# Value rows in idle strips, a later normaliser step and a weight piece in a place of its own

## The chip, the cores and the metric

The kernel runs on one core of one Trainium2 chip. The metric is the device time of one execution in microseconds (us), lower is better. Engines are named as in the profile: PE (TensorE, matrix products), DVE (VectorE), ACT (ScalarE), POOL (GpSimd) and SP (SyncE, which issues nearly all DMAs). Each engine takes its instructions in the order of its own program; an instruction waits on semaphores that other engines and DMAs raise.

## The reference

One inference step of a one-layer decoder with 1,024 channels. A prompt of 512 tokens and 8 single sample tokens go through the same weights, 520 columns in all. One wide projection feeds a matrix-memory branch (mLSTM, four heads, key width 128, value width 256) and a sliding-window attention branch; both are gated and merged, projected, normalised, and go through a SwiGLU feed-forward block and a second normalisation.

```
z = x @ w_in                      # qk, mv, gates i/f, mo, aq, ak, av, gm, ga
qk = silu(causal_dwconv(qk, state_conv));  q, k = split(qk)
C_new = decay * C + i * k v^T;   n_new = decay * n + i * k     # per head
h = (q C) / max(|q n|, exp(-m)); h = rmsnorm(h)
y_m = sigmoid(mo) * h * g;       y_a = window_attention(aq, ak, av, sinks)
x = LN(ALPHA x + (sigmoid(gm) y_m + sigmoid(ga) y_a) @ w_out)
g, u = split(x @ w_gate_up);     ffn = (silu(g) * u) @ w_down
y = LN(ALPHA x + ffn + sigmoid(x @ w_ple_gate) * (p @ w_ple))
```

The prompt starts from an empty state and is done in chunks. Each of the 8 sample tokens has a state matrix C (128 x 256 for each head) and a normaliser n that are read, updated and written back; the convolution rows and the window caches are outputs too.

## The kernel before

Activations lie transposed, channels on partitions, 520 columns of which the first 8 are the samples. Every fp32 product is three matmuls: operands are split into a high and a low part (`split`: the high part by ACT at L218, the low part by DVE or POOL at L219), and high x high, high x low and low x high are summed in PSUM (L245). Weights come in blocks of up to 1 MB into a ring `raw` of two; each piece of a block (`prep_next`, L189) is split into the rings `whi` and `wlo`, three buffers each, unless `dest` names a place for it.

The projection runs in steps t, each 128 output channels: 48 matmuls on PE, then an evacuation. Steps 0 to 7 are the convolved q and k, 8 to 15 the memory values (`ev_mv`), 16 and 17 attention keys and values, 18 to 25 attention queries, then the gates. `ev_mv` copies a value block into the ring `stg` of two buffers of 520 columns (ACT, L984), transposes it on PE (L987, L992), and copies the prompt part (DVE, L988) and the sample part (L996) out of PSUM; after every second block it stores the sample rows to a scratch tensor `vsd` in DRAM (SP, L998).

Work beside the projection is queued in `sd`: `sd.add(steps, a, b)` spreads steps over t = a to b. What matters here:

- `conv_out` (L967), t 8 to 10: transposes the eleven convolution rows, copies them into two `stg` buffers and stores them with four DMAs (L974, L975).
- `smlstm_prep` (L1095), t 8 to 10: the sample normaliser. It reads n, transposes it (L1099), waits for `wdb`, a broadcast of gate factors through DRAM (L913), forms the new normaliser on DVE (L1102 to L1106), transposes it back (L1109), copies (L1111) and stores it (L1113).
- `ml0` to `ml3`: the prompt's memory. `ml0` broadcasts gate rows into the strips S0 to S7 (520 columns each, two for each head); `ml1` reads them in an exponential (ACT, L1054). When the last head's exponentials are done the strips are idle.
- `sm0`, `sm1`, `sm2`: sample states, eight groups (h, g) of four states of head h. `sm0` reads the states (L1120) and the broadcast value rows from `vsd` (L1121, 512 KB) into two buffers of the ring `big` (four buffers, shared with attention and other work). `sm1` scales the value rows by the key (ACT, L1141), adds the decayed state (DVE, L1142), splits the result, and multiplies it by the query on PE (L1148); SP stores the new states (L1152).
- `at1` to `at3`, `sattn`: window attention, on the same engines at the same time.

The feed-forward part begins with two column blocks of `w_gate_up` that are used directly, in eight pieces `k_gu` to `k_gu + 7`; pieces 3 and 4 have places of their own in a late tile, the others use the rings. The first pieces run while the first normalisation is finished, over half of the columns and then over the other half (the loop over `pb4`); beside the end of that loop DVE and ACT form sums of rows and their splits `tf` (L1490 to L1496) for the next stage.

The program is written in this order, but each engine's order is set by a scheduler that simulates the program as it is written; `tc.issue_after` (in `after`, L448) holds a step's instructions behind a named one.

Of the kernel before, what the change touches and what calls it, by code (L numbers as in the profile page):

```python
# [17 lines left out]
P = 128  # L18
# [32 lines left out]
def tile_hybrid_step(  # L51
# [915 lines left out]
    def conv_out():  # L967
        for g in range(2):
            ps = pss()
            for i in range(4):  # L970
                T.transpose(ps[:11, i * P : (i + 1) * P], cvo[:, 4 * g + i, :], ident)
            ost = ring("stg", NT, 2)
            V.tensor_copy(ost[:11, :512], ps[:11, :])
            nc.sync.dma_start(o_convs[0, :, 2, g * 512 : (g + 1) * 512], ost[:NS, :512])  # L974
            nc.sync.dma_start(o_convp[0, 0, :, g * 512 : (g + 1) * 512], ost[NS:11, :512])  # L975
            yield
# [4 lines left out]
    def ev_mv(f, pss2):  # L981
# [6 lines left out]
        V.tensor_copy(  # L988
            vaug()[:, :, f // 2, (f % 2) * P : (f % 2 + 1) * P], ps.rearrange("p (c d) -> p c d", c=NCH)
        )  # L990
# [125 lines left out]
    def sm0(hg):  # L1116
        h, g = hg
        Ct = big()[:, :1024].rearrange("p (b d) -> p b d", b=4)
        vb = big()[:, :1024].rearrange("p (b d) -> p b d", b=4)
        nc.sync.dma_start(Ct, st_C[0, 4 * g : 4 * g + 4, h].rearrange("b k d -> k b d"))  # L1120
        nc.sync.dma_start(  # L1121
            vb, vsd[4 * g : 4 * g + 4, h * DV : (h + 1) * DV].partition_broadcast(P)
        )
        late_t["sm", hg] = (Ct, vb)

    def sm1(hg):
# [12 lines left out]
        for i in range(4):  # L1139
            b = 4 * g + i  # L1140
            S.activation(vb[:, i, :], vb[:, i, :], AF.Copy, scale=kws[:, h, b : b + 1])  # L1141
            V.scalar_tensor_tensor(  # L1142
                Ct[:, i, :], Ct[:, i, :], wdb[:, h, 1, b : b + 1], vb[:, i, :], ALU.mult, ALU.add
            )
            cc = [ring("gt", 264, 5)[:, :DV] for _ in range(2)]
            split(cc[0], cc[1], Ct[:, i, :], G)
            for x in range(2):
                T.matmul(  # L1148
                    pn[:40, :DV], rr(qz[:, b, :]), rr(cc[x]),
                    start=(b == 0 and x == 0), stop=(b == NS - 1 and x == 1),  # L1150
                )
# [26 lines left out]
    mxhi = []  # L1178
    mxlo = []

    def ev_ga(f, pss2):
        if f == 0:
            mxhi.extend(v3(slab(3)))
# [37 lines left out]
    sd.add(gen_steps(smlstm_prep()), t_mv, t_mv + 2)  # L1221
# [63 lines left out]
    dest[k_gu + 4] = (sub8(T6, 2), sub8(T6, 3))  # L1285

# [134 lines left out]
    with tc.manual_schedule(engines={E.PE, E.DVE, E.Pool, E.Activation}):  # L1421
# [40 lines left out]
        ts[4, 0] = ev_g(pg[4], n0)  # L1462
        c1, n1 = HALVES[1]
# [555 lines left out]
```

## Time and profile before

| | before |
|---|---|
| median of 3 runs | 884.36 us (882.98 to 884.54) |
| profiled execution, its own time | 885.6 us |
| its span | 883.5 us (2.1 us lie around it) |
| mean granted PE clock | 0.995 |
| PE busy | 866.0 us (98%), 7,082 matmuls |
| DVE, ACT, POOL busy | 659.4, 475.5, 156.2 us |
| DMA | 103.69 MB, 117 GB/s over the span |

All busy times and stretches come from one profiled execution. A timeline row gives the start, the time that a run of like instructions took, the engine, line and operation, and in brackets the idle time of that engine just before and what ended it. Matmuls overlap, so the 0.28 us of one says little; 48 of the projection's matmuls take 5.76 us, 0.12 us each. What an engine other than PE waits for costs time only where PE then waits for it.

### The profile page before, as it was taken

How to read it: one execution, taken by the hardware profiler on the slowest of the kernel's cores; microseconds unless marked ns; L12 is line 12 of the kernel's file. 1: busy time of each engine (PE TensorE's matmuls, PEld its weight loads, DVE VectorE, ACT ScalarE, POOL GpSimd, SP SyncE). 2: the span in 40 equal slices, each digit the busy share in tenths (PEclk: the TensorE clock that was granted, in tenths of full speed). 3: DMA queues.
4: the chain of work that ended last, by engine and by line, in shares of the span. 5: the costliest groups of instructions: out<-in, count | busy, mean ns of one | idle time of the engine just before them, and what ended most of it. 6: DMA issues, size and time to landing. Idle time of an engine off the chain costs nothing.

```text
span 883.5 us, 18583 instructions
## 1 busy us (share of the span) xinstructions
PE 866.0 (98%) x7082; PEld 853.2 (97%) x7082; DVE 659.4 (75%) x1589; ACT 475.5 (54%) x1131; POOL 156.2 (18%) x315
## 2 busy tenths in 40 slices
PE   8999899999999999999999999999999999999996
PEld 7999899999999899999999999999999999999996
DVE  7788555688978676778876968898898875566337
ACT  6545254658777655566525846666666565222120
POOL 5441321115464411221012300000000000000002
PEclk9999999999999999999999999999999999999998
DMA  7642631336465451131520043333334337634212
GB/s 244 223 145 73 194 102 55 55 106 145 157 180 172 145 143 49 49 97 48 191 97 1 23 111 104 112 108 97 107 101 116 108 115 219 202 120 150 96 37 97
DMA packets 125369, 103.69 MB, mean 117 GB/s; under 512 B 7210, under 2 KB 121090, under 8 KB 125256
## 3 DMA queue, kind: packets, MB, share of 16 engines
q1 hardware_dynamic: 125136, 102.38, 38.7%
q8 instruction: 55, 0.90, 0.4%
q14 instruction: 34, 0.28, 0.1%
q10 hardware_dynamic: 144, 0.13, 0.0%
HBM read 91.14 MB, written 12.47 MB: 117 GB/s over the span
## 4 chain that ended last, share of the span: by engine, by line
PE 87%; DVE 5%; DMA 3%; ACT 2%; issue 1%; POOL 1%; SPq 0%; DVEq 0%; ACTq 0%
PE psm L245 41%; PE psm L1601 14%; PE pss L1601 11%; PE psm L228 5%; PE psm L1894 2%; PE psm L1918 2%; PE pss L684 2%; PE pss L737 1%; PE pss L721 1%; PE psm L1429 1%; DMA big<-vsd 1%; PE psm L468 1%; PE pss L1070 1%; PE pss L1074 1%; DMA wdb<-bcd 1%
## 5 line engine op out<-in xcount | busy, mean ns | idle before, releaser
L245 PE MATMUL psm<-T,whi 128*128 128x264 f32 (+1 forms) x1728 | 301.9, 287 | 0.2 <-ACT th L1169 0.2
L245 PEld LDWEIGHTS psm<-T,whi 128*128 128x128 f32 x1728 | 246.8, 189 | 2.1 <-ACT th L1169 0.5
L245 PE MATMUL psm<-T,wlo 128*128 128x256 f32 (+1 forms) x912 | 200.1, 288 | 1.5 <-DVE wlo L219 1.5
L245 PEld LDWEIGHTS psm<-T,wlo 128*128 128x128 f32 x912 | 145.7, 189 | 2.5 <-DVE wlo L219 1.9
L219 DVE TENSOR_TENSOR wlo<-raw,whi 128x1024 fp32r<-128x1024 f32 (+2 forms) x75 | 90.5, 1207 | 66.8 <-ACT whi L218 66.7
L218 ACT ACTIVATE whi<-raw 128x1024 fp32r<-128x1024 f32 (+2 forms) x75 | 77.2, 1034 | 96.9 <-PE psm L245 79.5
L1784 POOL COPY amaskA<-tmp 128x8 f32<-128x8 f32 x8 | 1.5, 189 | 362.9 <-DVE tmp L1782 362.8
L709 POOL TENSOR_SCALAR g<-g,sm 128x256 f32<-128x256 f32 (+1 forms) x64 | 36.2, 579 | 80.2 <-DVE sm L707 23.8
L1585 DVE TENSOR_TENSOR whi<-raw,whi 128x512 fp32r<-128x512 f32 x55 | 37.8, 688 | 11.6 <-ACT whi L1580 10.7
L1580 ACT ACTIVATE whi<-raw 128x512 fp32r<-128x512 f32 x55 | 34.6, 628 | 19.5 <-PE psm L1601 14.4
L1580 ACT ACTIVATE wlo<-raw 128x512 fp32r<-128x512 f32 x55 | 34.6, 629 | 16.3 <-ACT gt L1619 10.2
L1585 DVE TENSOR_TENSOR wlo<-raw,wlo 128x512 fp32r<-128x512 f32 x55 | 37.8, 687 | 6.0 <-ACT wlo L1580 5.6
L702 ACT ACTIVATE g<-g,sm 128x256 f32<-128x256 f32 (+1 forms) x64 | 30.2, 474 | 18.7 <-DVE sm L698 17.7
L245 PE MATMUL psm<-L,whi 128*128 128x264 f32 x192 | 38.7, 282 | 0.0
L219 POOL TENSOR_TENSOR gt<-big,gt 128x256 fp32r<-128x256 f32 x32 | 27.7, 873 | 51.3 <-ACT gt L218 39.5
L1601 PE MATMUL psm<-tf,whi 128*128 128x260 f32 x276 | 36.7, 282 | 0.0
L1601 PE MATMUL psm<-T,wlo 128*128 128x260 f32 x264 | 35.3, 283 | 0.0
L1601 PE MATMUL pss<-tf,whi 128*128 128x260 f32 x264 | 35.3, 283 | 0.0
L1601 PE MATMUL pss<-tf,wlo 128*128 128x260 f32 x264 | 35.3, 283 | 0.0
L1601 PE MATMUL psm<-T,whi 128*128 128x260 f32 x264 | 35.3, 283 | 0.0
L1601 PEld LDWEIGHTS psm<-tf,whi 128*128 128x128 f32 x276 | 34.5, 188 | 0.0
L1601 PE MATMUL psm<-tf,wlo 128*128 128x260 f32 x252 | 33.5, 282 | 0.0
(461 smaller groups left out, 2104.3 us busy)
## 6 DMA issues: line engine op xcount, KB each, us to landing
raw<-in_w_in_dram SPq DMA_DIRECT2D x24, 1024.0 KB
raw<-in_w_gate_up_dram SPq DMA_DIRECT2D x72, 256.0 KB
raw<-in_w_down_dram SPq DMA_DIRECT2D x8, 1024.0 KB
big<-in_state_mlstm_C_dram SPq DMA_DIRECT2D x8, 512.0 KB
big<-vsd SPq DMA_DIRECT2D x8, 512.0 KB
out_dram<-big SPq DMA_DIRECT2D x8, 512.0 KB
raw<-in_w_out_dram SPq DMA_DIRECT2D x4, 1024.0 KB
raw<-in_w_gate_up_dram SPq DMA_DIRECT2D x4, 1024.0 KB
```

Source lines behind the costliest of these rows:

```text
L218: S.activation(rr(hi), src, AF.Copy)
L219: (le or V).tensor_tensor(rr(lo), src, hi, ALU.subtract)
L228: T.matmul(ps[:, :n], rr(w[:, k, wc : wc + P]), rr(a[k0 + k][:, c0 : c0 + n]), start=(i == 0), stop=(i == tot - 1),)
L245: T.matmul(ps[:, :n], rr(w[:, k, wc : wc + P]), rr(a[k0 + k][:, c0 : c0 + n]), start=(i == 0), stop=(i == tot - 1),)
L684: T.matmul(sc[:, a, :w], rr(q[:, a, n * P : (n + 1) * P]), rr(KS[:, kv, hl, (n - 1 + k0) * P : (n + 1) * P]), start=(hl == 0), stop=(hl == 1),
L702: S.activation(pr[:, a, :w], pr[:, a, :w], AF.Exp, bias=sm[:, 2 + a : 3 + a], scale=ASC, accum_out=sm[:, 8 + a : 9 + a],)
L709: G.tensor_scalar(pr[:, a, :w], pr[:, a, :w], sm[:, 12 + a : 13 + a], 0.5, ALU.mult, ALU.mult)
L1580: S.activation(rr(t[:, 0]), wsrcs[i], AF.Copy)
L1585: V.tensor_tensor(rr(lo), wsrcs.pop(i), hi, ALU.subtract)
L1601: T.matmul(ps[:, :TH], rr(w[:, j, :]), rr(x[j]), start=(start and j == 0 and i == 0), stop=(j == 3 and i == 2), skip_group_check=not start,)
L1894: T.matmul(pA[a][:, :264], rr(w[:, a * P : (a + 1) * P]), rr(x[:, :264]), start=(j == 0 and i == 0), stop=(j == KF - 1 and i == 2),)
L1918: T.matmul(pC[c][:, :256], rr(hk[k][x][:, t0 : t0 + P]), rr(w), start=(k == 0 and i == 0), stop=(k == KF - 1 and i == 2),)
```

## The change

Four edits:

- `conv_out` copies its rows into the ring `g2` (five buffers of 512 columns, shared with attention and `ml1`) instead of `stg`.
- The three steps of `smlstm_prep` go from t 8 to 10 to t 10 and 11, and are held behind the latest prompt copy of `ev_mv` (L988).
- `sm0` reads the value rows in two halves of two states, 256 KB each. For heads 0 and 1 both halves lie in one `big` buffer as before; for heads 2 and 3, the last four groups, they lie in the strips 4 and 5 (g = 0) or 6 and 7 (g = 1).
- Gate-up piece 5 gets a place of its own, in the end of the slab that holds the merged activations and in the end of a late tile, and `prep_next()` is called once more ahead of the `pb4` loop.

```
@@ conv_out
-            ost = ring("stg", NT, 2)
+            ost = g2()
@@ ev_mv
-        V.tensor_copy(
+        late_t["mv"] = V.tensor_copy(
             vaug()[:, :, f // 2, (f % 2) * P : (f % 2 + 1) * P], ps.rearrange("p (c d) -> p c d", c=NCH)
-        )
+        ).ins
@@ sm0
-        vb = big()[:, :1024].rearrange("p (b d) -> p b d", b=4)
         nc.sync.dma_start(Ct, st_C[0, 4 * g : 4 * g + 4, h].rearrange("b k d -> k b d"))
-        nc.sync.dma_start(
-            vb, vsd[4 * g : 4 * g + 4, h * DV : (h + 1) * DV].partition_broadcast(P)
-        )
+        vb = []
+        for i in range(2):
+            if 2 * h + g >= 4:
+                v2 = strip(4 + 2 * g + i)[:, :512].rearrange("p (b d) -> p b d", b=2)
+            else:
+                if i == 0:
+                    vb4 = big()
+                v2 = vb4[:, 512 * i : 512 * i + 512].rearrange("p (b d) -> p b d", b=2)
+            b0 = 4 * g + 2 * i
+            nc.sync.dma_start(v2, vsd[b0 : b0 + 2, h * DV : (h + 1) * DV].partition_broadcast(P))
+            vb += [v2[:, 0], v2[:, 1]]
@@ side queue
-    sd.add(gen_steps(smlstm_prep()), t_mv, t_mv + 2)
+    smp = smlstm_prep()
+    sd.add([lambda: after(next, smp, None, f_=[late_t["mv"]]) for _ in range(3)], t_mv + 2, t_mv + 3)
@@ gate-up pieces
+    dest[k_gu + 5] = tuple(
+        t[:, 6 * NT : 6 * NT + 1024].rearrange("p (k n) -> p k n", k=KD) for t in (mx3[0], T5[0])
+    )
...
         ts[4, 0] = ev_g(pg[4], n0)
+        prep_next()
         c1, n1 = HALVES[1]
```

The scheduler then moves instructions on every engine. Line numbers of the changed program are 7 to 14 higher from `sm0` on (L1121 is L1129, L1141 is L1148, L1142 is L1149, L1152 is L1159, L1496 is L1510).

The first place is DVE around the normaliser step (L1102 to L1106), near 100 us in the trace of before; `T_195` are the prompt's value rows, `tmp` the sample's.

```order
+L988 COPY T_195_1231<-pss_1377 128x4x128
+L996 COPY tmp_1298<-pss_1383 8x128
+L219 TENSOR_TENSOR wlo_1480<-raw_1165,whi_1479 128x1024
+L996 COPY tmp_1452<-pss_1450 8x128
+L988 COPY T_195_1231<-pss_1444 128x4x128
 L1102 TENSOR_TENSOR kws_574<-T_123_603,wdb_570 128x32
-L1104 TENSOR_TENSOR nst_575<-pss_1320,wdb_570 128x32
+L1104 TENSOR_TENSOR nst_575<-pss_1456,wdb_570 128x32
 L1103 TENSOR_SCALAR kws_574<-kws_574 128x32
 L1105 TENSOR_TENSOR nst_575<-nst_575,kws_574 128x32
```

The copies of two value blocks and a weight split now stand ahead of the step instead of behind it. On PE the transpose L1109 moves with it, from the place ahead of the second block's transposes to 31 matmuls behind the third block's; on ACT the four scalings of the first state group (L1148) now stand ahead of a weight split and of the fourth block's evacuation instead of behind both; on SP the store L998 and the two reads of that group's value rows stand ahead of the four stores L1113 and of a weight load.

The second place is ACT from about 196 us, before first and then the change; `QSa` are attention queries, `g` attention scores, `S_523` a strip.

```order
L1027 ACTIVATE T_123_603<-pss_2499,mgq_542 128x128 x2
L1015 ACTIVATE g_2487,hs_2489<-g_2487,hs_2489 128x256
L702 ACTIVATE g_2514,sm_2513<-g_2514,sm_2513 128x128 x2
L702 ACTIVATE g_2532,sm_2531<-g_2532,sm_2531 128x256
L700 ACTIVATE sm_2513<-sm_2513 128x2
L700 ACTIVATE sm_2531<-sm_2531 128x2
```

```order
L1027 ACTIVATE T_123_603<-pss_2499,mgq_542 128x128 x2
L702 ACTIVATE g_2515,sm_2514<-g_2515,sm_2514 128x128 x2
L1148 ACTIVATE S_523_3220<-S_523_3220,kws_574 128x256 x2
L702 ACTIVATE g_2533,sm_2532<-g_2533,sm_2532 128x256
L700 ACTIVATE sm_2514<-sm_2514 128x2
L702 ACTIVATE g_2533,sm_2532<-g_2533,sm_2532 128x256
```

A scaling of strip rows stands in the middle of the softmax scalings; two more pairs (`S_522`, `S_554`) stand earlier among the query copies L667, and a fourth (`S_555`) later. On PE three readers of what stands behind them (a transpose L1024, the scores L684 and a transpose L721) are 8, 8 and 15 matmuls further back than before.

The third place is DVE at the gate-up pieces near 502 us, before first; `wlo_7107` is piece 5's low part before, `L_5609<-raw_6714` the same in the change.

```order
L219 TENSOR_TENSOR L_5597<-tmp_6928,T_899_5657 128x264
L1496 SCALAR_TENSOR_TENSOR T_123_603<-T_123_603 128x260
L219 TENSOR_TENSOR tf_7050<-T_123_603,tf_7048 128x260
L219 TENSOR_TENSOR tf_7049<-T_123_603,tf_7047 128x260
L1496 SCALAR_TENSOR_TENSOR T_123_603<-T_123_603 128x260
L219 TENSOR_TENSOR tf_7049<-T_123_603,tf_7047 128x260
L219 TENSOR_TENSOR wlo_7107<-raw_6702,whi_7106 128x1024
```

```order
L219 TENSOR_TENSOR L_5609<-tmp_6940,T_903_5669 128x264
L1510 SCALAR_TENSOR_TENSOR T_123_603<-T_123_603 128x260
L219 TENSOR_TENSOR L_5609<-raw_6714,T_903_5669 128x1024
L1510 SCALAR_TENSOR_TENSOR T_123_603<-T_123_603 128x260
L219 TENSOR_TENSOR tf_7069<-T_123_603,tf_7067 128x260
L219 TENSOR_TENSOR tf_7068<-T_123_603,tf_7066 128x260 x2
```

Piece 5's low part stands four instructions earlier. Its high part stands on ACT right behind the same SiLU gate as before's two `tf` splits of 499 us, ahead of them.

More of the change, by code (lines that the diff above doesn't have):

```diff
@@ L1140, in sm1 @@
             b = 4 * g + i
-            S.activation(vb[:, i, :], vb[:, i, :], AF.Copy, scale=kws[:, h, b : b + 1])
+            S.activation(vb[i], vb[i], AF.Copy, scale=kws[:, h, b : b + 1])
             V.scalar_tensor_tensor(
-                Ct[:, i, :], Ct[:, i, :], wdb[:, h, 1, b : b + 1], vb[:, i, :], ALU.mult, ALU.add
+                Ct[:, i, :], Ct[:, i, :], wdb[:, h, 1, b : b + 1], vb[i], ALU.mult, ALU.add
             )
@@ L1178, in tile_hybrid_step @@
     mxhi = []
+    mx3 = []
     mxlo = []
@@ L1182, in ev_ga @@
         if f == 0:
-            mxhi.extend(v3(slab(3)))
+            mx3.append(slab(3))
+            mxhi.extend(v3(mx3[0]))
         ms = []
```

## The prediction

> **What bounds the kernel now.** I read the page's busy times and its chain first, then a table of stretches, then the timelines of the stretches in which TensorE is not full.
>
> ```profile
> PE 866.0 (98%) x7082; PEld 853.2 (97%) x7082; DVE 659.4 (75%) x1589; ACT 475.5 (54%) x1131; POOL 156.2 (18%) x315
> ...
> PE 87%; DVE 5%; DMA 3%; ACT 2%; issue 1%; POOL 1%; SPq 0%; DVEq 0%; ACTq 0%
> ```
>
> TensorE is busy for 866.0 of 883.5 us and carries 87% of the chain. The change removes no TensorE work, so all that it can win lies in 17.5 us of idle time and in slow clock. The next table says where those are; its columns are the stretch, its length, the busy time of PE, PEld, DVE, ACT and POOL, the granted clock, and the DMA share and rate.
>
> ```profile
> 0.00:27.00 27.00, 23.46 (x146) 19.88 (x147) 18.52 (x45) 16.21 (x30) 14.28 (x30) 1.00 0.78 247
> 100.00:120.00 20.00, 17.55 (x135) 17.22 (x134) 8.96 (x23) 7.38 (x16) 4.71 (x7) 0.91 0.54 163
> 120.00:290.00 170.00, 169.87 (x1358) 166.10 (x1357) 130.22 (x418) 115.59 (x337) 59.60 (x131) 1.00 0.45 120
> 290.00:310.00 20.00, 18.14 (x143) 16.76 (x142) 13.44 (x37) 12.15 (x36) 8.67 (x13) 1.00 0.47 151
> 500.00:506.00 6.00, 4.48 (x38) 4.27 (x38) 6.00 (x15) 5.11 (x10) 0.00 (x0) 1.00 0.00 0
> 103.40:106.80 3.40, 3.40 (x18) 3.32 (x17) 2.33 (x4) 1.61 (x3) 2.49 (x4) 0.51 0.64 163
> ```
>
> The change cannot reach the start. It touches the three stretches that lose 2.45 (100 to 120), 1.86 (290 to 310) and 1.52 us (500 to 506), 5.83 us in all. The last row adds one more: for 3.4 us behind the first of these gaps the granted clock is 0.51, and half of that, 3.40 x 0.49 = 1.67 us, is lost without any idle time. Together 7.5 us, or 0.85%, is the most that I can point to.
>
> **Around 100 us: normaliser step and value rows.** Rows of TensorE, VectorE, ScalarE and of the chain:
>
> ```profile
> 100.24 0.40 PE L245 MATMUL psm<-T,whi 128*128 128x264 f32 x2
> 103.08 0.27 PE L1109 MATMUL pss<-ident,nst 128*32 128x128 f32 x1 [2.45 <-DVE nst L1105]
> 102.30 0.19 DVE L1102 TENSOR_TENSOR kws<-T,wdb 128x32 f32<-128x32 f32 x1 [2.06 <-DMA wdb<-bcd]
> 95.47 6.74 DMA wdb<-bcd
> 97.94 1.04 ACT L218 ACTIVATE whi<-raw 128x1024 fp32r<-128x1024 f32 x1
> 102.51 0.66 ACT L984 ACTIVATE stg<-psm 128x264 f32<-128x264 f32 x2 [3.52 <-DVE kws L1102]
> ```
>
> A 6.74 us broadcast holds VectorE at L1102, and TensorE, in program order, sits at the transpose L1109 behind it. In the changed order L1102 to L1106 stand behind two more sets of value copies, and the transpose 31 matmuls later still. TensorE writes the second set 47 matmuls, 5.6 us, behind the first (99.4, below), so L1102 comes at some 106 us, and the broadcast has landed at 95.47 + 6.74 = 102.21. So 2.45 us goes, and the 1.67 us of clock with it.
>
> What is late next is the evacuation of the second value block (L984). It stood at 102.51; the trace puts that down to VectorE, but its two `stg` buffers were then still being stored by the conv rows. With the conv rows in another ring it can run right behind the weight split, at 97.94 + 1.04 = 98.98; with 0.33 us for half of the 0.66, TensorE can transpose at about 99.4. It reaches those transposes 13 matmuls ahead of the point where it stood at 103.08 - 2.45 = 100.63, and without L1099: at 0.12 us a matmul (170 us would hold 1,417 of them) 98.8 to 99.1. A new gap of 0.3 to 0.6 us; I take 0.6. It is far below 2.45, so I charge no clock. Conv rows in the other ring cost nothing I can find: same copies, same stores, five buffers instead of two.
>
> The moved step also changes ScalarE: the four scalings of the first value group now stand ahead of a weight split and of the fourth block's evacuation. Prices, and the landing they wait for:
>
> ```profile
> L1141 ACT ACTIVATE big<-big,kws x32: 492/495/512, 113.6 to 297.6; 128x256 f32<-128x256 f32 x32
> 103.69 1.48 SPq L1113 DMA_DIRECT2D out_dram<-tmp  x4
> 105.28 0.27 SPq L998 DMA_DIRECT2D vsd<-tmp  x1
> ...
> 107.23 0.39 SPq L1121 DMA_DIRECT2D big<-vsd  x1
> ...
> 217.85 0.37 SPq L1121 DMA_DIRECT2D big<-vsd  x1
> 223.88 0.51 ACT L1141 ACTIVATE big<-big,kws 128x256 f32<-128x256 f32 x1 [1.76 <-DMA big<-vsd]
> ```
>
> The sample store L998 moves ahead of the four L1113 stores (1.48 us) and its reads ahead of a weight load, so they should be issued near 105 instead of 107.23. One read of 512 KB took 223.88 - 217.85 = 6.0 us; two of half the size ahead of the weight load I estimate at 3.5 to 6, landing at 108.5 to 111. Behind that come four scalings (some 1.7), a split (1.04) and half an evacuation (0.33), 3.1 us. TensorE needs the result 47 + 55 matmuls and ten small ones behind 99.4, near 113. So the margin is between +1.4 and -1.1 us. I take zero cost and keep 1 us for the range. L1113's stores now wait behind the state store on SP; nobody reads them. Net of this part: 4.1 - 0.6 = 3.5 us.
>
> **Around 290 to 307 us: value rows of the last groups.** ScalarE, TensorE, and ScalarE's waits from 180 to 310 us:
>
> ```profile
> 288.17 8.17 DMA big<-vsd
> 296.42 1.71 ACT L1141 ACTIVATE big<-big,kws 128x256 f32<-128x256 f32 x4 [5.37 <-DMA big<-vsd]
> 298.49 0.51 PE L737 MATMUL pss<-big,VS 128*128 128x256 f32 x2 [1.48 <-ACT T L1027]
> 301.25 0.51 PE L245 MATMUL psm<-T,whi 128*128 128x256 f32 x2 [0.22 <-ACT th L1169]
> 306.61 0.33 PE L721 MATMUL pss<-ident,g 128*128 128x128 f32 x1 [0.16 <-POOL g L709]
> ACT big L1141 <- DMA big<-vsd: 11.9, 7, 5.4
> ```
>
> The last group's value rows take 8.17 us, ScalarE stands 5.37 us with everything behind it, and TensorE loses 1.48 + 0.22 + 0.16 = 1.86 us. After the change these rows are read into strips that come free near 265 us and are scaled, by the order, near 275, ahead of this place. What is late next is the state tile of the same group, which is loaded as before; I expect it about 5 us ahead of TensorE's use. So 1.86 us goes.
>
> The reads of the fifth and sixth group move into 184 to 215 us, and their scalings too, in line on ScalarE (those of the seventh and eighth follow near 255 to 275, when the same strips are free again). They start when the last exponentials free the strips; the first row is a stretch of the table above, with DMA share 0.00:
>
> ```profile
> 184.00:193.00 9.00, 9.00 (x68) 8.69 (x67) 7.07 (x24) 5.50 (x17) 1.56 (x3) 1.00 0.00 0
> 184.02 0.39 ACT L1054 ACTIVATE g<-S,colI 128x128 f32<-128x128 f32 x1
> 189.09 0.39 ACT L1054 ACTIVATE g<-S,colI 128x128 f32<-128x128 f32 x1
> 198.47 0.40 ACT L702 ACTIVATE g<-g,sm 128x128 f32<-128x128 f32 x1 [0.95 <-DVE sm L698]
> ```
>
> By the order against these rows, reads issue near 184.4, 189.5 and 195 and ScalarE comes to their scalings near 186, 192 and 199; the fourth comes later, at 215. The first two find the DMA engines idle; at the 3.5 us estimated above ScalarE stands 2 and 1 us. The third is queued behind a 1 MB weight load and could hold it 2 to 3. Queued behind are the query copies L667, the transposed gates L1027 and the softmax scalings L702, all feeding TensorE. How much reaches TensorE no row shows directly. The nearest: of the seven waits of this kind (11.9 us), the six short ones, 11.9 - 5.4 = 6.5 us, lie almost all in 120 to 290, where TensorE idles 0.13 us. The long one let through 1.86 of 5.37. So the bounds are 0 and 2.5 us; the waits are of the short kind and the scheduler moved TensorE's readers 8 to 15 matmuls (1 to 1.8 us) back, so I take 0.5. Eight more reads at some 0.4 us of issue cost SP 3 us beside work that waits for none of it. Net: 1.86 - 0.5 = 1.4 us.
>
> **Around 503 us: one gate-up piece.** TensorE, VectorE and ScalarE:
>
> ```profile
> 503.10 0.40 PE L245 MATMUL psm<-T,whi 128*128 128x264 f32 x2
> 505.02 0.39 PE L245 MATMUL psm<-T,wlo 128*128 128x264 f32 x1 [1.52 <-DVE wlo L219]
> 502.06 0.42 DVE L1496 SCALAR_TENSOR_TENSOR T<-T 128x260 f32<-128x260 f32 x1
> 502.40 0.76 DVE L219 TENSOR_TENSOR tf<-T,tf 128x260 fp32r<-128x260 f32 x2
> 503.76 1.21 DVE L219 TENSOR_TENSOR wlo<-raw,whi 128x1024 fp32r<-128x1024 f32 x1
> 499.03 0.90 ACT L218 ACTIVATE tf<-T 128x260 fp32r<-128x260 f32 x2
> 500.86 1.05 ACT L218 ACTIVATE whi<-raw 128x1024 fp32r<-128x1024 f32 x1
> ```
>
> TensorE wants the low part at about 503.3 and gets it at 503.76 + 1.21 = 504.97, because the piece had to wait for a ring buffer. With a place of its own its high part stands on ScalarE ahead of the two `tf` rows of 499.03 and its low part on VectorE right behind the row of 502.06. It then starts at 502.40 instead of 503.76, 1.36 us sooner, and ends at 503.6. The high part pushes those `tf` rows by 1 us; VectorE reads them only from about 500.4, so I charge 0.1. Net 1.3 us of 1.52; bounds 0 and 1.52. The `tf` low parts that slip behind it are wanted at 522 us.
>
> **The sum.** 3.5 + 1.4 + 1.3 = 6.2 us. The profiled execution took 885.6 us (span 883.5, 2.1 around it), so 879.4 by its own time. The median of the three runs is 884.36, 1.2 below; the same gain gives 878.2 us.
>
> **A rule against a row.** The gap of 2.45 us is followed at once by half clock; the gaps of 1.48 and 1.52 us are not. The Trainium skill, "TensorE: Matmul & The Clock Gate", section "HAM oscillation — how this bites in real kernels", has as its rule that idle gaps up to about 3.4 us do no harm to the clock. By that rule the 2.45 us gap is not what halved it, the 1.67 us would stay, and the sum would be 4.5. I go by the row: it is the only gap of its size here, and the slow stretch starts where it ends.
>
> **The rivals.**
> (1) The value rows of the first group land late (111 us or more): ScalarE holds the fourth block, TensorE loses 1 us or more near 113 and as much again at the strips. Gain 6.2 - 2.0 = 4.2, 880.2 us. For it: the 8.17 us read; against it: two smaller reads ahead of the weight load. 0.18.
> (2) Slower: ScalarE stands at the strip reads from 186 to 207 as it stood at 291, because such reads take long wherever they stand. With 7 us from issue (between the 6.0 and the 8.17 of the rows) the waits are 184.4 + 7 - 186 = 5.4, then 4.5 and 3.0; less 1.8 us of moved readers each, TensorE idles 3.6, 2.7 and 1.2 us, 7.5 in all, and twice over 2.45, so the clock halves twice (3.3). Lost 10.8, won 6.7 (the 6.2 without the 0.5 charged): 4.1 slower, 888.5 us. It decides from a read of some 6 us on. Against it: DMA engines idle there, half the bytes, six waits that cost nothing. 0.08.
> (3) Piece five is no earlier, because VectorE is never idle there and the `tf` rows come late: 6.2 - 1.3 = 4.9, 879.5 us. 0.14.
> (4) The clock stays halved for 3.4 us though the gap goes (the rule above, or because the new gap at 99 is larger than I think): 6.2 - 1.7 = 4.5, 879.9 us. 0.12.
> (5) The change does not do what it says: new waits of about the old size take the place of the three. 884.4 us. 0.06.
> My forecast has 0.42.
>
> **How the numbers follow.** The low end is all three gaps and the clock, 7.5 us, with a little more where starts lie further apart than the idle time says: 8.4 us, 876.0. The high end takes rivals 1, 3 and 4 and part of their mixtures, 2.0 us of gain, 882.4. About 0.2% (1.8 us) is what a measurement of this kernel can tell from no change. Faster by more holds the forecast, 1, 3 and 4 (0.86, less mixtures of them: 0.84); within it falls rival 5 and some mixtures, 0.08; slower is rival 2, 0.08.
>
> **What would show it.** Right: L1109 without idle time before it and no half clock from 103 to 107; less than 1 us of idle time before the value transposes; no ScalarE wait near 291 on value rows; the low part of piece five starting on VectorE before TensorE asks. Wrong: idle time of TensorE over 0.5 us in 185 to 250 with a ScalarE wait on a strip read behind it, or a second stretch of half clock.

## The result and the profile after

The changed kernel takes 892.01 us (median of 5 runs, 890.57 to 893.88); the kernel before, in the same measurement, takes 884.54 us (882.98 to 887.01). The ratio is 1.0085, with an interval of 1.0064 to 1.0106: the change makes the kernel slower by about 7.5 us, where 6 us of gain was forecast. Ratios and their 95% intervals, here and below, leave out a few executions of over 1,190 us, which the medians include, and can differ a little from the ratio of two medians. The profiled execution of the changed kernel took 893.88 us by its own time (span 891.9 us).

First the page's busy times and the shares of its chain.

```profile
PE 868.7 (97%) x7082; PEld 856.2 (96%) x7082; DVE 662.9 (74%) x1589; ACT 475.6 (53%) x1131; POOL 159.5 (18%) x315
...
PE 84%; DVE 7%; DMA 3%; ACT 3%; issue 2%; POOL 1%; SPq 0%; DVEq 0%; ACTq 0%
```

TensorE's share of the chain fell from 87% to 84%, and its idle time rose from 17.5 to 891.9 - 868.7 = 23.2 us. The table of stretches, in the same columns as before, says where:

```profile
100.00:120.00 20.00, 18.56 (x154) 17.99 (x154) 10.14 (x23) 7.98 (x18) 7.63 (x14) 1.00 0.65 200
185.00:207.00 22.00, 20.74 (x164) 20.18 (x162) 12.43 (x50) 10.38 (x32) 2.11 (x4) 1.00 0.50 128
207.00:230.00 23.00, 16.66 (x109) 15.59 (x110) 14.97 (x47) 15.48 (x44) 7.68 (x11) 0.87 0.53 100
301.00:321.00 20.00, 19.79 (x165) 19.21 (x164) 18.15 (x55) 13.90 (x41) 10.01 (x13) 1.00 0.40 119
210.20:213.60 3.40, 3.40 (x11) 2.64 (x12) 2.79 (x7) 2.11 (x7) 2.07 (x3) 0.51 0.00 0
227.30:230.70 3.40, 3.40 (x18) 3.33 (x18) 2.93 (x9) 3.38 (x12) 2.84 (x4) 0.50 1.07 373
```

Three of the four places went the way they were meant to: 100 to 120 us loses 1.44 us instead of 2.45 and has full clock; the work of 290 to 310, which runs some 11 us later here, at 301 to 321, loses 0.21 instead of 1.86; and the gap of 1.52 us at the gate-up piece is down to 0.16 (the row at 513.21 below). But in 185 to 230 us, where TensorE was full before, it is now idle 1.26 + 6.34 = 7.60 us, and two stretches of 3.4 us at half clock follow, 3.40 x 0.49 + 3.40 x 0.50 = 3.4 us more: 11 us that were not there before. TensorE also starts 3.2 us later than in the profile of before; that varies from one execution to another, as the unchanged kernel shows further on.

The timeline of that place: the four strip scalings on ScalarE, then TensorE's two gaps, then what SP issued.

```profile
189.06 0.91 ACT L1148 ACTIVATE S<-S,kws 128x256 f32<-128x256 f32 x2 [2.08 <-DMA S<-vsd]
...
194.87 0.51 ACT L1148 ACTIVATE S<-S,kws 128x256 f32<-128x256 f32 x1 [0.72 <-DMA S<-vsd]
...
207.59 0.91 ACT L1148 ACTIVATE S<-S,kws 128x256 f32<-128x256 f32 x2 [5.59 <-issue]
...
225.28 0.91 ACT L1148 ACTIVATE S<-S,kws 128x256 f32<-128x256 f32 x2 [5.13 <-DMA S<-vsd]
```

```profile
210.10 0.38 PE L721 MATMUL pss<-ident,g 128*128 128x128 f32 x1 [4.36 <-POOL g L709]
...
227.08 0.31 PE L1155 MATMUL pss<-gt,qz 128*40 128x256 f32 x1 [3.24 <-ACT gt L218]
```

```profile
195.68 0.37 SPq L165 DMA_DIRECT2D raw<-in_w_in_dram  x1
197.44 0.36 SPq L1084 DMA_DIRECT2D out_dram<-Cst  x1
197.84 0.43 SPq L1085 DMA_DIRECT2D out_dram<-Cst  x1
198.36 0.39 SPq L1129 DMA_DIRECT2D S<-vsd  x1
...
215.21 0.43 SPq L1085 DMA_DIRECT2D out_dram<-Cst  x1
215.74 0.40 SPq L1129 DMA_DIRECT2D S<-vsd  x1
```

The first two reads cost ScalarE 2.08 and 0.72 us, about what was forecast (2 and 1), and TensorE nothing. The third was issued at 198.36 and ScalarE starts on it at 207.59; the fourth at 215.74 and 225.28. Both are 256 KB, like the first two, and both took over 9 us. The row at 207.59 names "issue" and not the DMA: no releaser was recorded for it, but the semaphore events of the trace have that read complete at 207.5, so it is the same wait as in the row at 225.28. What stands in line on ScalarE behind the third is the softmax scalings L702, from which POOL makes `g` for the transpose L721: TensorE's gap of 4.36 us. Behind the fourth stand the splits `gt` that TensorE's L1155 wants: 3.24 us.

What the two slow reads have in common stands directly ahead of them in SP's queue. When the last chunk of a head is done, VectorE's update of the state (L1078) is also the last reader of that head's strip, so the same event lets SP store the head's results and refill the strip. L1084 stores the state, and L1085 the normaliser: one column, 128 packets of 4 bytes, 0.5 KB in all. By the semaphore events the store issued at 197.84 is complete at 207.3 us, 9.5 us for 512 bytes.

### The profile page after: what moved, and what is told of

Read it like the earlier page. It is cut to its first block, busy times and chain, and to the rows that moved or that the text cites. A ratio compares the mean times of both kernels' runs of the same rounds, so it can differ in the third digit from the quotient of the medians.

```text
span 891.9 us, 18606 instructions
## 1 busy us (share of the span) xinstructions
PE 868.7 (97%) x7082; PEld 856.2 (96%) x7082; DVE 662.9 (74%) x1589; ACT 475.6 (53%) x1131; POOL 159.5 (18%) x315
## 4 chain that ended last, share of the span: by engine, by line
PE 84%; DVE 7%; DMA 3%; ACT 3%; issue 2%; POOL 1%; SPq 0%; DVEq 0%; ACTq 0%
PE psm L245 39%; PE psm L1615 14%; PE pss L1615 10%; PE psm L228 5%; PE psm L1908 2%; PE psm L1932 2%; PE psm L468 1%; PE pss L737 1%; PE pss L684 1%; PE pss L721 1%; PE psm L1442 1%; DMA S<-vsd 1%; DMA raw<-in_w_down_dram 1%; PE pss L1070 1%; ACT T L1385 1%
## 5 line engine op out<-in xcount | busy, mean ns | idle before, releaser
L245 PE MATMUL psm<-T,whi 128*128 128x264 f32 (+1 forms) x1696 | 298.6, 287 | 0.0
L245 PEld LDWEIGHTS psm<-T,whi 128*128 128x128 f32 x1696 | 243.3, 189 | 1.6
L245 PE MATMUL psm<-T,wlo 128*128 128x256 f32 (+1 forms) x896 | 193.2, 286 | 0.3 <-DVE wlo L219 0.3
L245 PEld LDWEIGHTS psm<-T,wlo 128*128 128x128 f32 x896 | 142.4, 189 | 1.1 <-DVE wlo L219 0.5
L219 DVE TENSOR_TENSOR wlo<-raw,whi 128x1024 fp32r<-128x1024 f32 (+1 forms) x74 | 90.2, 1220 | 67.9 <-ACT whi L218 67.1
L218 ACT ACTIVATE whi<-raw 128x1024 fp32r<-128x1024 f32 (+1 forms) x74 | 76.1, 1033 | 92.1 <-PE psm L245 74.8
L1599 DVE TENSOR_TENSOR whi<-raw,whi 128x512 fp32r<-128x512 f32 x55 | 37.8, 687 | 11.4 <-ACT whi L1594 10.5
L702 ACT ACTIVATE g<-g,sm 128x256 f32<-128x256 f32 (+1 forms) x64 | 30.1, 474 | 17.9 <-DVE sm L698 17.7
```

Of the source, the lines that this page charges most:

```text
L218: S.activation(rr(hi), src, AF.Copy)
L219: (le or V).tensor_tensor(rr(lo), src, hi, ALU.subtract)
L245: T.matmul(ps[:, :n], rr(w[:, k, wc : wc + P]), rr(a[k0 + k][:, c0 : c0 + n]), start=(i == 0), stop=(i == tot - 1),)
L702: S.activation(pr[:, a, :w], pr[:, a, :w], AF.Exp, bias=sm[:, 2 + a : 3 + a], scale=ASC, accum_out=sm[:, 8 + a : 9 + a],)
L1599: V.tensor_tensor(rr(lo), wsrcs.pop(i), hi, ALU.subtract)
```

## The experiments

The theory after this reading has two halves. *The store*: L1085 makes the read behind it take 9 us instead of 3 or 4. *The line*: ScalarE takes the scaling in program order, so that a late read stops the softmax and with it TensorE. The rivals: such a read is slow there whatever stands ahead of it (a 1 MB weight load is in flight too); SP's queue, and not the DMA engines, is what the store blocks; the loss is not the strips' but that of another edit. The expectations give numbers for these. The kernels below ran in three sets of four, each set on one chip with the kernel before beside it, whose median was 885.61 us for the first four, 884.43 for the next four and 885.55 for the last four.

**Without the strips.** All edits but those to the value rows, which are read as before.

```
-        vb = []
-        for i in range(2):
-            ...
+        vb4 = big()[:, :1024].rearrange("p (b d) -> p b d", b=4)
+        nc.sync.dma_start(vb4, vsd[4 * g : 4 * g + 4, h * DV : (h + 1) * DV].partition_broadcast(P))
+        vb = [vb4[:, i] for i in range(4)]
```

> The change without its strip edit: value rows of all eight groups lie in a big buffer again, the other edits stay. Store theory (the third and fourth strip reads stand behind the 4-byte normaliser store L1085, ScalarE waits 5.6 and 5.1 us, TensorE idles 4.4 and 3.2 us and its clock halves twice): the 9.8 us lost from 200 to 230 us are gone, and so are the 1.8 us won at 290 to 310; about 881 us, no TensorE gap over 2 us from 185 to 250. Bandwidth theory (such reads are slow in that stretch whatever stands ahead of them): the same, about 881. Reorder theory (the other moved work makes the new gaps): about 892.

Measured: 882.73 us, ratio 0.9968 (0.9952 to 0.9984), where about 881 was expected. Its stretches:

```profile
207.00:230.00 23.00, 22.65 (x190) 22.22 (x189) 20.38 (x66) 18.90 (x54) 11.46 (x30) 1.00 0.40 116
290.00:310.00 20.00, 19.61 (x157) 18.43 (x156) 15.26 (x45) 13.31 (x38) 9.21 (x13) 1.00 0.48 156
```

From 207 to 230 TensorE loses 0.35 us instead of 6.34, at full clock, and the 1.26 us before it are gone as well: the loss is the strips'. And 290 to 310 loses only 0.39 us without them. That doesn't show that the other edits took the rest: a second profile of the unchanged kernel, further down, loses only 0.50 us there.

**The strips alone.** The kernel before with the edit to `sm0` only.

```
 (conv_out, ev_mv, smlstm_prep and the gate-up pieces as before; sm0 as in the change)
```

> The kernel before with the strip edit alone. Store theory and bandwidth theory: 884.5 + 9.8 - 1.8, about 892 us, with the two ScalarE waits of over 5 us before L1148 and two half-clock stretches of TensorE. Reorder theory: 884 or less, no such waits.

Measured: 897.91 us, ratio 1.014 (1.0116 to 1.0165), worse than the whole change, and than the 892 us that were expected. ScalarE's waits for strips from 183 to 290 us (total, times, longest), then TensorE's row at 104 us and the stretch that follows:

```profile
ACT S L1148 <- DMA S<-vsd: 16.5, 7, 5.2
```

```profile
103.70 0.27 PE L1109 MATMUL pss<-ident,nst 128*32 128x128 f32 x1 [2.15 <-DVE nst L1105]
```

```profile
104.80:108.20 3.40, 3.40 (x18) 3.40 (x18) 2.42 (x3) 1.06 (x3) 2.69 (x4) 0.50 0.44 116
```

The strips by themselves lose about 12 us. The gap ahead of L1109 is there as before, here 2.15 us, and 3.4 us of half clock follow it here too.

**The normaliser as a row.** The whole change, but the column is transposed on TensorE and stored as one row of 512 bytes.

```
-            nc.sync.dma_start(o_np[0, 0, h].unsqueeze(1), C[:, DV : DV + 1], ...)
+            ps = pss()
+            T.transpose(ps[:1, :P], C[:, DV : DV + 1], ident)
+            nrow = ring("tmp", 264, 4)
+            V.tensor_copy(nrow[:1, :P], ps[:1, :P])
+            nc.sync.dma_start(o_np[0, 0, h].unsqueeze(0), nrow[:1, :P])
```

> The change with the normaliser column of each head (L1085, 128 packets of 4 bytes) transposed on TensorE and stored as one row of 512 bytes. Store theory: the reads behind it land 3 to 5 us after issue instead of 9.2 and 9.5, ScalarE waits under 2 us before L1148, and the time is 892 less about 9, 880 to 884 us. Bandwidth theory: the reads still take 7 us or more beside the 1 MB and 512 KB transfers, 888 to 892 us. Reorder theory: about 892.

Measured: 885.05 us, ratio 1.0004 (0.9985 to 1.0022): the loss is gone, the gain is not there; 880 to 884 us were expected. SP's rows of the third read, then ScalarE's third and fourth scaling:

```profile
197.15 0.48 SPq L1133 DMA_DIRECT2D S<-vsd  x1
199.50 0.26 SPq L1089 DMA_DIRECT2D out_dram<-tmp  x1
```

```profile
201.61 0.91 ACT L1152 ACTIVATE S<-S,kws 128x256 f32<-128x256 f32 x2 [1.99 <-DMA S<-vsd]
...
213.67 0.91 ACT L1152 ACTIVATE S<-S,kws 128x256 f32<-128x256 f32 x2 [0.23 <-DMA S<-vsd]
```

```profile
185.00:207.00 22.00, 21.85 (x168) 20.90 (x167) 13.92 (x53) 14.02 (x44) 3.74 (x8) 1.00 0.43 137
207.00:232.00 25.00, 24.33 (x206) 23.92 (x205) 23.51 (x70) 21.83 (x63) 13.60 (x30) 1.00 0.56 173
```

The third read is ready 201.61 - 197.15 = 4.5 us after issue instead of 9.2, and TensorE loses 0.82 us in the two stretches instead of 7.60. But this kernel changes two things at once: the store is one packet, and it is issued behind the read (199.50), since the row has to be made first. The next two kernels take these apart.

**The store on another queue.** The whole change with L1085 issued by ScalarE.

```
-            nc.sync.dma_start(o_np[0, 0, h].unsqueeze(1), ...)
+            nc.scalar.dma_start(o_np[0, 0, h].unsqueeze(1), ...)
```

> The change with the 4-byte store L1085 issued on ScalarE's DMA queue instead of SyncE's; SyncE's order is otherwise the same. Store theory in the form that order within SyncE's queue is what holds the reads: reads in 3 to 5 us, 880 to 884 us. Store theory in the form that the 4-byte packets hold the shared DMA engines whichever queue they come from: reads of 7 us or more, 888 to 893 us. Bandwidth theory: about 892.

Measured: 891.0 us, ratio 1.0065 (1.0041 to 1.009).

```profile
197.30 0.36 ACTq L1085 DMA_DIRECT2D out_dram<-Cst  x1
197.75 0.39 SPq L1129 DMA_DIRECT2D S<-vsd  x1
...
207.78 0.91 ACT L1148 ACTIVATE S<-S,kws 128x256 f32<-128x256 f32 x2 [5.95 <-issue]
...
210.30 0.47 PE L721 MATMUL pss<-ident,g 128*128 128x128 f32 x1 [4.46 <-POOL g L709]
```

SP's queue is free of the store, and the read issued at 197.75 is ready at 207.78, 10.0 us, as slow as before. So it is not SP's queue that the 4-byte packets hold up; they hold up the transfers behind them wherever they were issued. The Trainium skill, "DMA: Bandwidth & Descriptors", section "Issuing engines are not separate DMA queues", says that DMAs started by different engines run on the same 16 DMA engines and interleave there, and that another issuing engine saves only its own issue time. These rows agree: 9.2 us from the one queue, 10.0 from the other.

**A quarter of the packets.** The whole change with only 32 of the 128 values of each head's normaliser stored (96 are left out); place and queue are the same.

```
-            nc.sync.dma_start(o_np[0, 0, h].unsqueeze(1), C[:, DV : DV + 1], ...)
+            nc.sync.dma_start(o_np[0, 0, h, : P // 4].unsqueeze(1), C[: P // 4, DV : DV + 1], ...)
```

> The change with L1085 storing only the first 32 of the 128 normaliser values of each head (96 are left out), 32 packets of 4 bytes instead of 128. Packet theory (the store's time goes with its number of 4-byte packets): the reads behind it land about 6 us sooner, ScalarE waits under 2 us at the third and fourth strip read, and the time is 882 to 887 us. If the store has a fixed price whatever its length, or the reads are slow for another reason: ScalarE waits 5 us as before, 890 to 893 us.

Measured in one execution: 883.76 us, 8.3 us below the changed kernel's median (the kernel before beside the two: 884.43 and 884.54).

```profile
194.67 0.42 SPq L1085 DMA_DIRECT2D out_dram<-Cst  x1
195.19 0.38 SPq L1129 DMA_DIRECT2D S<-vsd  x1
...
201.27 0.91 ACT L1148 ACTIVATE S<-S,kws 128x256 f32<-128x256 f32 x2 [2.41 <-issue]
...
203.79 0.33 PE L721 MATMUL pss<-ident,g 128*128 128x128 f32 x1 [0.95 <-POOL g L709]
```

With 32 packets in the same place the read is ready 201.27 - 195.19 = 6.1 us after issue instead of 9.2, ScalarE waits 2.41 us instead of 5.59, and TensorE 0.95 us instead of 4.36. That is some 3 us sooner, where 6 was expected, but the time of the read goes with the number of 4-byte packets ahead of it: that half of the theory is shown, in one execution, without the change of order that the row kernel had. The 1 MB weight load is not what makes the difference: here too it is issued 2.7 us ahead of the third read, and in the changed kernel the fourth read, which has none ahead of it, is as slow as the third. Nor is it the state store L1084, which stands ahead of the read in both kernels: ahead of the changed kernel's fourth read it is complete at 216.55 us and L1085 only at 225.0, by the semaphore events.

**The line.** The whole change, store and reads as they are, but each strip scaling is held behind the scalings of the group before, so that it doesn't stand among the softmax scalings.

```
+                if 2 * h + g >= 4:
+                    hold.enter_context(tc.issue_after(late_t["sc"]))
+                sc = S.activation(vb[i], vb[i], AF.Copy, scale=...)
+        late_t["sc"] = sc.ins
```

> The change, with each scaling of strip rows queued on ScalarE behind the scalings of the group before it; the reads into the strips stay where they are. In-line theory (what costs is ScalarE standing at L1148 with query copies and softmax behind it, not the slow read itself): the third and fourth read still take 9 us or more, no ScalarE wait over 1 us at strip rows before 240, no TensorE gap over 2 us from 185 to 250, and 879 to 883 us. Transfer theory (the slow stretch of the DMA engines also delays weights and states that TensorE needs): 887 to 892 us with gaps of another origin at 205 to 230.

Measured: 895.7 us, ratio 1.0125 (1.0105 to 1.0145): slower still. The stretches say why:

```profile
185.00:207.00 22.00, 22.00 (x172) 21.40 (x172) 16.13 (x63) 13.72 (x44) 5.39 (x10) 1.00 0.56 144
207.00:232.00 25.00, 23.61 (x194) 22.57 (x193) 22.00 (x64) 19.70 (x55) 11.44 (x29) 1.00 0.48 138
400.00:440.00 40.00, 35.01 (x258) 33.47 (x257) 30.15 (x93) 23.89 (x68) 6.50 (x10) 0.87 0.22 71
```

The reads stand behind the store as ever, and the third and fourth are complete 9.0 and 8.0 us after issue by the semaphore events, yet 185 to 232 loses 1.39 us instead of 7.60: where nothing stands in line behind the scaling, the slow read costs little. That bears out the second half of the theory, as far as a kernel with another order can. The time went the wrong way because the scheduler, given other constraints, put the end of attention elsewhere (the last transpose L721 is at 426.2 us, in the kernel before at 413.6), and 400 to 440 us now loses 4.99 us and stays at half clock for some 10. The forecast of this kernel's time was wrong for a reason that none of the theories held.

**The last head only.** The same, with strips for the last two groups alone (`>= 6` for `>= 4` in `sm0`).

> As the run before, but only the last head's two groups use the strips; the fifth and sixth group have big buffers again. In-line theory: 878 to 882 us, no value-row wait near 291 and none at 200 to 230. Transfer theory: 887 us or more.

Measured: 884.47 us, ratio 1.0001 (0.9985 to 1.0017): neither loss nor gain, where 878 to 882 was expected. The slow reads are still there, and not only those into strips: the ordinary value rows that SP issues behind the store, at 195.11 and 195.65, take 12.7 and 14.2 us by the semaphore events. ScalarE waits 2.44 and 1.19 us for them, and TensorE loses 2.59 us from 207 to 232. What else keeps the gain away is not shown.

**The kernel before, once more.** One more execution of the unchanged kernel, for what differs between executions.

```
 (no edit)
```

> The kernel before, unaltered, profiled once more, to see how far its start-up differs between executions. If the 3.2 us that the changed kernel is late at 31 us belong to the change, TensorE's 49th projection matmul starts at 31.2 us as in the first profile; if they are a matter of the execution, it starts up to 3 us later here too.

Measured: 884.87 us. The row answers to the 2.45 us of the first profile, and the stretches to that profile's 17.55 us at 0.91 and 18.14 us:

```profile
104.27 0.27 PE L1109 MATMUL pss<-ident,nst 128*32 128x128 f32 x1 [2.11 <-DVE nst L1105]
```

```profile
100.00:120.00 20.00, 17.89 (x149) 17.56 (x149) 10.41 (x24) 8.34 (x19) 5.00 (x8) 1.00 0.58 177
290.00:310.00 20.00, 19.50 (x155) 18.09 (x154) 14.43 (x40) 12.99 (x37) 9.21 (x13) 1.00 0.49 157
```

Here the same projection matmul comes 1.50 us later at 31 us than in the first profile of this kernel, with nothing changed. Over all profiles of this study that start is between 0.1 us earlier and 3.7 later; the changed kernel's was 3.2 later. A late start shortens the gap ahead of L1109, since the broadcast it waits for does not come later by as much: 2.45 us, 2.11 here, and 1.24 in the profile of the piece-only kernel below. And the clock stays full behind 2.11 us. The loss of 1.86 us from 290 to 310 is down to 0.50 with nothing changed, too.

With the late start goes slow clock: it is half from 24.4 to 27.8 us in this profile, from 8.9 to 12.3 and from 25.9 to 29.3 in the changed kernel's, and nowhere before 100 us in the first one. How much of the delay that makes is not shown.

**The edits one by one, without strips.** Three kernels: the gate-up piece alone on the kernel before; the normaliser step and the conv ring alone; and everything but the strips with the value rows still read in halves.

```
 (first: only mx3, dest[k_gu + 5] and prep_next())
 (second: only g2() in conv_out, late_t["mv"] and the held smlstm_prep)
 (third, on the change:)
-            if 2 * h + g >= 4:
+            if 2 * h + g >= 8:
```

> The kernel before with gate-up piece 5 in its own place and the one earlier call of prep_next, nothing else. By the changed kernel's trace (TensorE 9.54 us behind the kernel before at 503 us and 8.18 behind at 505) the gap before the low part falls by 1.36 us: 884.5 - 1.4, about 883. If VectorE had been the bound there (rival 3), 884.5.

> The kernel before with the conv rows in the other ring and the later normaliser step, nothing else. The gap of 2.45 us and, where it follows, the half clock behind it go, and the 1.44 us gap before the second block's transposes comes: 884.5 less 1 to 2.5, 882 to 883.5. My first sum had 3.5 for this part, 881.

> The change with every group's value rows in a big buffer, still read in two halves of 256 KB: all of the change but the strips. As the run without the strip edit (882.7), and less the 0.6 us gap that its one 512 KB read left at 115: 881.5 to 883.

Measured: the piece 883.08 us, ratio 0.9983 (0.9965 to 1.0001); the normaliser step 883.88 us, 0.9987 (0.9972 to 1.0001), a little over the 882 to 883.5 expected; all but the strips 882.01 us, 0.9959 (0.9942 to 0.9976). The last is clear: 0.41% of 885.55 is 3.6 us, with 2.1 to 5.1 as the interval. The two parts, 1.5 and 1.2 us, are each just short of telling apart from nothing. Against the first profile of the kernel before, that of the piece's kernel gains 1.35 us between 503 and 505 us. Of the kernel with all but the strips, the stretch in which the strips were to help; it loses 1.11 us there:

```profile
290.00:310.00 20.00, 18.89 (x153) 17.77 (x152) 13.83 (x40) 12.58 (x37) 8.23 (x13) 1.00 0.50 145
```

**The new gap at 100 us.** In the changed kernel and in the last two of these TensorE waits 1.42 to 1.44 us for the copy L984. The rows of the changed kernel:

```profile
101.67 0.40 ACT L1054 ACTIVATE g<-S,colI 128x128 f32<-128x128 f32 x1 [4.43 <-POOL S L1040]
...
102.93 0.64 ACT L984 ACTIVATE stg<-psm 128x264 f32<-128x264 f32 x2
...
103.35 0.71 PE L987 MATMUL pss<-ident,stg 128*128 128x128 f32 x4 [1.44 <-ACT stg L984]
```

ScalarE stands 4.43 us at an exponential whose mask POOL adds late, with the weight split and the copy in line behind it. So one more kernel: all but the strips, with these exponentials (L1054) held behind the copy.

```
-            S.activation(vT[:, c0 : c0 + n], psx[:, :n], AF.Copy)
+            late_t["ev", f] = S.activation(vT[:, c0 : c0 + n], psx[:, :n], AF.Copy).ins
...
-        S.activation(E, bm[:, a0 : a0 + P], AF.Exp, bias=colI[:, c, h : h + 1])
+        with tc.issue_after(late_t["ev", 1]):
+            S.activation(E, bm[:, a0 : a0 + P], AF.Exp, bias=colI[:, c, h : h + 1])
```

> The kernel of the run before with the prompt memory's first exponentials (L1054) queued on ScalarE behind the second value block's copy (L984) instead of ahead of the weight split in front of it. If the 1.44 us gap there comes of ScalarE waiting in line for GpSimd's mask adds at the exponential, it goes: 1.4 us below the run before, 880 to 881.5. If the copy is late for another reason, no difference.

Measured: 881.31 us, ratio 0.9956 (0.9939 to 0.9973), the fastest kernel here and faster than both the kernel before and the change.

```profile
99.38 0.64 ACT L984 ACTIVATE stg<-psm 128x264 f32<-128x264 f32 x2
```

```profile
100.00:120.00 20.00, 19.78 (x165) 19.22 (x164) 9.36 (x23) 7.56 (x18) 8.38 (x16) 1.00 0.67 204
```

The copy runs at 99.38 and the stretch loses 0.22 us instead of 1.42. That the gap goes is shown; that it is worth time is not, since the two kernels are 0.7 us apart and their intervals overlap.

## Why the prediction was wrong

**The step that failed** is the price of the strip reads at 186 to 215 us. The prediction said of them that the third "is queued behind a 1 MB weight load and could hold it 2 to 3", that "the fourth comes later, at 215", and took 0.5 us for all, with bounds of 0 and 2.5. The third and fourth held ScalarE 5.59 and 5.13 us, and TensorE lost 7.60 us and 3.4 us of clock. Three things went wrong in it. The queue ahead of the read was looked at only for bytes: the 0.5 KB store L1085 stands directly ahead of it, because the event that frees the strip is the one that releases the store. The price was taken from one read (217.85, 6.0 us) which has no such store right ahead of it, though earlier in the trace of before there is one that has:

```profile
195.64 0.46 SPq L1085 DMA_DIRECT2D out_dram<-Cst  x1
196.20 0.48 SPq L1120 DMA_DIRECT2D big<-in_state_mlstm_C_dram  x1
196.73 0.62 SPq L1121 DMA_DIRECT2D big<-vsd  x1
```

```profile
208.53 1.71 ACT L1141 ACTIVATE big<-big,kws 128x256 f32<-128x256 f32 x4 [0.77 <-DMA big<-vsd]
```

That read was ready 11.8 us after its issue, behind the store and a state read, and cost nothing only because ScalarE came to it late. And the fourth read was named but not priced. Both signs of being wrong that the prediction gave came about: idle time in 185 to 250 us behind a strip read, and a second stretch of half clock.

**The rival that held half of the mechanism** was the second, at a chance of 0.08: ScalarE stands in line at the strip reads, TensorE idles behind it and its clock halves twice. Its reason, that "such reads take long wherever they stand", is not what the runs show, for the first two took 3.4 and 3.1 us. Its price for the clock (3.3 us) was right. Its sum of idle time came out (7.5 us against 7.60) by luck: it had the first three reads at 7 us each, and it was the third and fourth at 9.2 and 9.5, the first two being as short as the forecast had them. Its point of decision, a read of some 6 us, fits the quarter kernel, whose 6.1 us read costs TensorE 0.95. By it the change would have been 4.1 us slower, 10.8 lost and 6.7 won; measured are 11 lost there and 3.6 won by all but the strips, 7.4 in all, against 7.5 in the medians. One reason for its small chance, "DMA engines idle there", holds for the first two reads alone.

**Around 100 us** (3.5 us forecast). The gap at L1109 and the half clock behind it went, as forecast. The new gap at the transposes is 1.44 us, not 0.6: the copy L984 does not follow the weight split at 98.98, because an exponential stands in line ahead of the split and waits for POOL, which the prediction did not look at. And the 4.1 us to be won were those of one execution: in a second profile of the same kernel the gap is 2.11 us and the clock full behind it, so that 2.1 us is all there is in that execution. The edit alone measured 1.2 us, with -0.1 to 2.5 as the interval. The first rival, value rows late near 113, did not come about: the gap at the transposes is all that the changed kernel loses from 100 to 120 us (20.00 - 18.56 = 1.44).

**Around 290 us** (1.86 us forecast from the strips). In the changed kernel ScalarE waits 0.60 and 1.38 us for these value rows (at 286.4 and 290.3 us) instead of 5.37, and TensorE loses 0.21 us at 301 to 321. But the two kernels of all edits but the strips lose only 0.39 and 1.11 us there, and the unchanged kernel 0.50 in its second profile. So the 1.86 us, like the gap at L1109, were those of one execution, and the strips bring 0.9 us at most.

**The gate-up piece** (1.3 us forecast). Right, with its reason, as far as one wait goes. VectorE and TensorE of the changed kernel:

```profile
511.61 0.42 DVE L1510 SCALAR_TENSOR_TENSOR T<-T 128x260 f32<-128x260 f32 x1
511.95 1.21 DVE L219 TENSOR_TENSOR L<-raw,T 128x1024 fp32r<-128x1024 f32 x1
```

```profile
513.21 0.39 PE L245 MATMUL psm<-T,L 128*128 128x264 f32 x1 [0.16 <-DVE L L219]
```

The low part follows the row it was said to follow, and TensorE waits 0.16 us where it waited 1.52. The edit alone measured 1.5 us, with -0.1 to 3.1 as the interval. The third rival, by which the piece is no earlier, is out.

**The rule against the row.** The prediction went by the gap of 2.45 us that was followed by half clock, against the rule of the Trainium skill ("TensorE: Matmul & The Clock Gate", section "HAM oscillation — how this bites in real kernels") that gaps up to about 3.4 us do no harm. The other profiles agree with the row and not with the rule: gaps of 2.15, 2.46 and 3.24 us were followed by half clock too, as were those of 4.36 and 4.46, where the rule has it so.

Yet one of 2.11 us was not, and in the strips-only kernel half clock also followed a gap of 1.41 us. What the half clock goes with in these traces is not the length of a gap alone. Within each profile all changes of the granted clock lie whole multiples of 3.413 us apart, which divides the time into fixed windows. From 30 to 850 us of the 14 profiles there are ten windows at full clock in which TensorE idles 1.91 us or more, and half clock follows each of them in the next window; it follows none of the others, which idle 1.53 us at most. The gap of 2.45 us lay in one window, 100.02 to 103.43. The gap of 2.11 us lay in two, 0.71 us in the first and 1.40 in the second. Of the gap of 1.41 us, 1.08 lay in the window before the half clock, and shorter gaps beside it make 1.91. The rows show the second window of the 2.11 us gap, then the window of the 1.41 us gap:

```profile
102.87:106.28 3.41, 2.01 (x17) 2.02 (x18) 1.70 (x8) 2.11 (x5) 0.79 (x2) 1.00 0.57 157
```

```profile
224.23:227.64 3.41, 1.50 (x8) 0.90 (x9) 2.47 (x8) 3.34 (x13) 1.61 (x3) 1.00 1.01 289
```

So the price of 1.67 us for the clock was right for that execution and no constant: a gap of some 2 us pays it or not by where it falls.

**The sum.** Against the first profile of before, by the same projection matmuls, the changed kernel's profile is 3.2 us late at 31 us, 0.75 late from 130 to 200 (the region of 100 us took 2.5 back, part of it only because a late start is absorbed there), 11.3 late at 290 (the strips, 10.5), 9.5 late at 400 (290 to 310 gave back 1.8, which that profile of before had lost there), and 8.2 late from 505 us on (the piece, 1.3). Without the strips the forecast would have been 3.5 + 1.3 = 4.8 us, and 3.6 (2.1 to 5.1) was measured.

**Open.** The strips with a quick store (the row kernel) bring no gain over the kernel before, though TensorE loses only 0.82 us at the strips there. Its median is 2.3 us above that of the first kernel without strips, on the same chip; the profiles don't show where these would lie, since the two profiled executions have nearly one span, 881.7 and 880.9 us. Four of the row kernel's twelve executions have spans of 884.6 to 886.7 us, more than any of the other kernel's (at most 882.8), and none of these four was profiled. A version with both the row and the held exponential was not tried.

## What to carry to other kernels

Before a read is put in a new place, look at what stands right ahead of it in the queue and what event releases both, and count packets there, not bytes: a column of 128 values, 0.5 KB, delayed a 256 KB read by about 6 us. Price a moved read by a row that has the same neighbours in its queue, and ask of each waiting instruction what stands in line behind it; idle DMA engines at the first two of four reads say nothing of the other two. A gain read from one execution's gap should be read from a second execution before it is counted.

## What the runs showed of the hardware

- A store of one column, 128 packets of 4 bytes, took 7.5 to 10.3 us in the five profiles that have a strip read behind it, and that read of 256 KB 8.0 to 11.7 us, on the same queue or on another. With 32 packets the third read took 6.1 us, with the store behind it 4.5. The changed kernel's first two reads, with no such store ahead, took 3.4 and 3.1 us (all complete by the semaphore events).
- The clock changes on a grid of 3.413 us. A window at full clock with 1.91 us or more of idle time was followed by one at half clock, and one with 1.53 us or less was not; a gap of 2.11 us across two windows passed at full clock.
- The same kernel starts up to 1.5 us later in one execution than in another (all kernels together: 3.8 us of spread), and a later wait can absorb it, so that a gap's size in one profile is no constant of the program.
